# Reloads of gates and o in the W_A stage of blocks 1 and 2 tied to the ends of products

## The chip, the cores and the metric

The kernel runs on one core of one Trainium2 chip. The metric is the time of one execution on the device, in microseconds (us). All times of single instructions come from one profiled execution, counted from the start of its span.

## What is computed

One layer of a hybrid encoder is applied to a prompt of 2048 tokens and to a sample of 64 tokens, with 1024 features each, in float32. What matters here is the end of the layer:

```python
yA = einsum(silu(zA) * bA * conv, w_a_out)           # stage W_A
o  = o * rsqrt(mean(o * o) + EPS) * g_onorm          # o: result of the recurrent scan
yB = einsum(o * silu(zB), w_b_out)                   # stage W_B
merged = sigmoid(gA) * yA + sigmoid(gB) * yB
out = einsum(merged, w_o)                            # stage W_O
x = x + rms_norm(out, g_post)
x = x + (p @ w_ple_proj) * sigmoid(rms_norm(x, g_ple) @ w_ple_gate)
```

Ahead of it stand one wide projection `h @ w_in` with ten parts (vA, bA, cA, zA, q, f, iv, zB, gA, gB), a short convolution and the scan. gA, gB and the gated o are computed early in a block and used late.

## The kernel before

The 2112 tokens are cut into three blocks of 704 (blocks 0, 1, 2), each into two halves of 352. Activations lie as feature by token: eight tiles of 128 x 704 make one operand of 1024 features. Every matmul is 128 x 128 by 128 x 352. To keep float32 accuracy each operand is split in a high and a low part, and each product is made of three matmuls (high by high, high by low, low by high); splits are a cast on ScalarE and a subtraction on VectorE (`split`, L184 and L185).

Large matrix products are made by a Strassen scheme (Winograd's form): a 2 x 2 arrangement of weight blocks and activation blocks, seven products instead of eight. In the W_A and W_B stages of blocks 1 and 2 (`merge_in_turn`, `in_turn`) the seven products are run one after the other, in the order of `IN_TURN`: product 0 is A11 by B11, then 1: A12 by B21, 2: S2 by T2, 3: S3 by T3, 4: A22 by T4, 5: S1 by T1, 6: S4 by B22. One product runs over four groups of output features (g = 0 to 3); each group takes four k-steps of three matmuls, so 12 matmuls in a group and 48 in a product. While product n runs, `prepare` splits the operands of product n + 1, one k-step after each group, in `operand_of`, which for T2 also makes the sums of the scheme in place (L404 to L408).

The weights of a group come by SyncE's queue: a raw block or one of the precomputed sums S (256 KB, L195) is loaded to one of 5 `raw` tiles and cast on ScalarE to its high part (4 `hi` tiles). The low part is either loaded as well (256 KB, L216, to one of 4 `lo` or 3 `s` tiles), or, for the blocks listed under `anew` (A11 and A12 of W_A, A11 of W_B), computed on chip by L184 and L185, always to a `lo` tile. A tile is free again when its last reader is done, so a load runs ahead of TensorE by as many groups as there are tiles.

Results of a product go to the sinks: `sink_a` multiplies by the reloaded gate gA (tiles `m`), `sink_b` by gB (tiles `mg`) and adds `m`. Sinks run at products 1, 4, 5 and 6. The gates gA and gB, o and some others were spilled to memory earlier in the block (8 tiles of 352 KB each) and are brought back by `reload` (L929 to L932), a DMA that GpSimd issues (its line is L931) into one of 52 ring tiles. `loads` says when: gA 0 to 3 ahead of product 0, gA 4 to 7 after product 0, all of o after product 2, all of gB after product 5 of W_A. o is the operand of W_B. "After" is a place in the program's text: a scheduler orders each engine's instructions by their estimated times, and semaphores keep only what the data and the tiles need. On the chip a reload starts as soon as GpSimd reaches it and its ring tile is free, whatever TensorE is at.

Engines take their instructions in order, each from a queue of its own. GpSimd (POOL) issues the reloads and the spills and does few small computations; SyncE (SP) issues the weight loads. Both kinds of transfer run on the same 16 DMA engines.

Of the kernel before, what the change touches and what calls it, by code (L numbers as in the profile page):

```python
# [20 lines left out]
KB = D // P  # L21
KH = KB // 2
# [9 lines left out]
VA, BA, CA, ZA, QQ, FF, IV, ZB, GA, GB = range(10)  # L32
W_A, W_B, W_O, W_G = 80, 88, 96, 104
# [49 lines left out]
def hybrid_step(  # L83
# [17 lines left out]
    V, A, G, T, SP = nc.vector, nc.scalar, nc.gpsimd, nc.tensor, nc.sync  # L101
# [17 lines left out]
    def rt(n=BN, dt=F32):  # L119
        t = ring.tile([P, BN + 4], dt, tag="r", name=nm("r"))  # L120
        return t if n is None else t[:, :n]
# [112 lines left out]
    last, hooks = [None], []  # L234

    def placed():

        return tc.issue_after(last[0]) if last[0] is not None else nullcontext()

    def hook():  # L240

        if hooks:
            step = hooks.pop(0)
            if step is not None:
                step()
# [131 lines left out]
    def half(t, h):  # L377
        return t[:, h * HN : (h + 1) * HN]

    def whole(x, y):  # L380

        if y is None:
            return x
        t = hf()
        V.tensor_tensor(t, x, y, ALU.add)
        return t
# [102 lines left out]
    def gemm_late(idxs, act, segs):  # L489

        ws = [load_w(i) for i in idxs]
        pss = [[ps_gemm() for _ in segs] for _ in idxs]
        for ks in (range(KB - 1), (KB - 1,)):
            with placed() if len(ks) == 1 else nullcontext():
                for row, w in zip(pss, ws):
                    for ps, s in zip(row, segs):
                        for k in ks:
                            mm3(ps, w, act, k, cols_of(s))
        return pss
# [37 lines left out]
    def spread(cols, n):  # L537

        pb = ps_attn()
        with placed():  # L540
            for i, o in tiles_of(n):
                T.matmul(pb[:, o : o + P], cols[:, i : i + 1].to_broadcast([P, P]), ident, start=True, stop=True)
        return pb[:, :n]
# [8 lines left out]
    def col_rstd(acc, n):  # L552

        pc = ps_attn()
        cols = cols_tile(n)
        with placed():
            for i, o in tiles_of(n):
                T.matmul(pc[:, i : i + 1], acc[:, o : o + P], ones, start=True, stop=True)
        rstd_of(pc[:, : cols.shape[1]], cols, 1.0 / D)
        return cols  # L560
# [365 lines left out]
            yield  # L926


    def reload(d):  # L929
        t = rt()  # L930
        G.dma_start(t, d)  # L931
        return t  # L932

    def merge(bl, a, kept, extra):

        segs = bl["segs"]
        ob, m, mg, loaded = [], [], [], {}

        def fetch(kind, j):
            if j < KB:  # L940
                loaded[kind, j] = reload(kept[kind, j])

        fetch(GA, 0)
        fetch("o", 0)
        for j, pss in enumerate(gemms(W_A, a, segs)):
            fetch(GA, j + 1)
            fetch("o", j + 1)
            if j == KB - 1:
                fetch(GB, 0)
            sg = loaded.pop((GA, j))  # L950
            for s, ps in zip(segs, pss):
                V.tensor_tensor(sg[:, cols_of(s)], ps, sg[:, cols_of(s)], ALU.mult)
            m.append(sg)
            ob.append(split_rt(loaded.pop(("o", j))))
            if j % 2:
                next(extra, None)
        for j, pss in enumerate(gemms(W_B, ob, segs)):
            fetch(GB, j + 1)
            sg = loaded.pop((GB, j))
            for s, ps in zip(segs, pss):  # L960
                V.tensor_tensor(sg[:, cols_of(s)], ps, sg[:, cols_of(s)], ALU.mult)
            V.tensor_tensor(sg, sg, m[j], ALU.add)  # L962
            mg.append(split_rt(sg))
            if j % 2:
                next(extra, None)
        return mg

    def merge_in_turn(a, kept, mg, made):

        ob, m = [], []  # L970

        def gated(v, x, y):
            V.tensor_tensor(v, whole(x, y), v, ALU.mult)

        def sink_a(g, c, h, x, y):
            gated(half(m[g + c * KH], h), x, y)

        def sink_b(g, c, h, x, y):
            j = g + c * KH
            gated(half(mg[j], h), x, y)  # L980
            V.tensor_tensor(half(mg[j], h), half(mg[j], h), half(m[j], h), ALU.add)
            made(j, h)

        def loads(idx, n):

            if (idx, n) in ((W_A, -1), (W_A, 0)):
                m.extend(reload(kept[GA, j]) for j in range(len(m), len(m) + KH))
            elif (idx, n) == (W_A, 2):
                ob.extend(reload(kept["o", j]) for j in range(KB))
            elif (idx, n) == (W_A, 5):  # L990
                mg.extend(reload(kept[GB, j]) for j in range(KB))

        return [
            dict(idx=W_A, raw=a, sink=sink_a, anew=("A11", "A12")),
            dict(idx=W_B, raw=ob, sink=sink_b, anew=("A11",)),
        ], loads
# [105 lines left out]
    for bi, bl in enumerate(blocks):  # L1102
        first, kept = bi == 0, kepts[bi]
# [24 lines left out]
        mg, xo, h2, acc = [], [], [], rt()  # L1128
        if first:
            mg = merge(bl, a, kept, sums_ahead)  # L1130
        else:
            parts = [None] * KB

            def made(j, h):

                if nxt:
                    if parts[j] is None:
                        parts[j] = rt(dt=F32R), rt(dt=F32R)
                    split(half(mg[j], h), *(half(t, h) for t in parts[j]))
# [12 lines left out]
            if nxt:  # L1152
                mg = parts
# [69 lines left out]
```

## Time and profile before

| What | us |
|---|---|
| median of 3 runs | 2730.09 |
| the three runs | 2727.76, 2732.46, 2730.09 |
| the profiled execution, its own time | 2728.34 |
| its span, first to last instruction | 2726.6 |
| mean granted clock of TensorE over the span | 0.987 |
| W_A of block 1, first matmul | 1584.33 |
| W_A of block 2, first matmul | 2450.47 |

How to read the lines below. In an order in time a line gives start, duration, engine, source line, operation, written and read tiles, shapes, count, and in brackets the idle time before it with what ended it. In a view by stretches, a line gives for each engine the busy time and the number of instructions, then TensorE's granted clock as a share of full speed, the mean busy share of the 16 DMA engines, and GB/s. In the DMA views, q0 is GpSimd's queue and q1 SyncE's; a line of issues has the count, the size of each and the median time from issue to landing. TensorE's matmuls are pipelined: their starts tell the pace, not their durations.

### The profile page before, as it was taken

To read this page: it belongs to the slowest core of one execution; us is meant where nothing else is said; L and a number is where in the kernel's file an instruction comes from. 1 tells how busy PE (TensorE), PEld (TensorE's weight loads), DVE (VectorE), ACT (ScalarE), POOL (GpSimd) and SP (SyncE) were. 2 spreads that over 40 slices of the span, in tenths; PEclk is the share of its full clock that TensorE was granted. 3 is DMA by queue.
4 is the path that set the end of the run, shared out by engine and by line. 5 is a ranking of instruction groups with operands and counts; after the bars stand their busy time and mean duration, and the time that the engine had idled before them with its cause. 6 is when DMAs were issued, how large, how long until landed. Compare 5 with 4: busy or idle time off the path is not lost.

```text
span 2726.6 us, 47857 instructions
## 1 busy us (share of the span) xinstructions
PE 2646.6 (97%) x16736; PEld 2610.7 (96%) x16736; DVE 1721.8 (63%) x3327; ACT 1457.9 (53%) x2796; POOL 367.9 (13%) x684
## 2 busy tenths in 40 slices
PE   6999999999999999999999999999999999999998
PEld 5999999999999999999999999999999999999988
DVE  6788888899666643566645567554355554357864
ACT  4665565454324553566654556454466654445654
POOL 1000001100332211011111210021010010010022
PEclk7999999999999999999999999999999999999999
DMA  5767777898988898766789998598866678888878
GB/s 200 268 239 275 260 243 278 280 314 291 346 312 288 305 340 271 243 224 223 232 279 335 390 335 259 180 349 306 268 224 219 217 225 269 272 290 305 280 240 313
DMA packets 365681, 748.90 MB, mean 275 GB/s; under 512 B 44704, under 2 KB 48320, under 8 KB 365440
## 3 DMA queue, kind: packets, MB, share of 16 engines
q1 hardware_dynamic: 325728, 589.84, 64.9%
q0 software_dynamic: 39424, 155.96, 15.6%
q8 instruction: 132, 2.16, 0.3%
q14 instruction: 109, 0.89, 0.1%
q10 hardware_dynamic: 288, 0.05, 0.0%
HBM read 538.29 MB, written 207.37 MB: 273 GB/s over the span
## 4 chain that ended last, share of the span: by engine, by line
PE 78%; DMA 8%; DVE 4%; issue 4%; ACT 2%; POOL 1%; SPq 0%; DVEq 0%; POOLq 0%; ACTq 0%
PE pg L345 17%; PE pg L346 17%; PE pg L347 17%; PE pg L472 3%; PE pg L473 3%; PE pg L471 3%; PE pg L438 3%; PE pg L439 3%; PE pg L440 3%; DMA raw<-w_blk 2%; DMA raw<-S 1%; PE pa L826 1%; PE pa L862 1%; PE pa L864 1%; PE pa L816 1%
## 5 line engine op out<-in xcount | busy, mean ns | idle before, releaser
L345 PE MATMUL pg<-r,hi 128*128 128x352 f32 x3360 | 1115.1, 333 | 15.9 <-ACT r L184 5.9
L346 PE MATMUL pg<-r,hi 128*128 128x352 f32 x3360 | 1090.4, 325 | 5.0 <-DVE r L185 5.0
L347 PE MATMUL pg<-r,lo 128*128 128x352 f32 x2400 | 779.9, 325 | 4.8 <-DMA lo<-low 3.5
L215 ACT CAST hi<-raw 128x512 fp32r<-128x512 f32 x740 | 455.9, 619 | 589.7 <-PE pg L346 216.3
L345 PEld LDWEIGHTS pg<-r,hi 128*128 128x128 f32 x3360 | 634.8, 189 | 26.8 <-ACT r L184 8.9
L346 PEld LDWEIGHTS pg<-r,hi 128*128 128x128 f32 x3360 | 635.6, 189 | 9.6 <-DVE r L185 9.5
L347 PEld LDWEIGHTS pg<-r,lo 128*128 128x128 f32 x2400 | 454.0, 189 | 7.0 <-DMA lo<-low 4.7
L347 PE MATMUL pg<-r,s 128*128 128x352 f32 x960 | 310.5, 324 | 0.4 <-DMA s<-low 0.3
L472 PE MATMUL pg<-r,hi 128*128 128x352 f32 x896 | 291.9, 326 | 2.6 <-DVE r L185 2.3
L471 PE MATMUL pg<-r,hi 128*128 128x352 f32 x896 | 290.3, 326 | 1.8 <-ACT r L184 1.7
L473 PE MATMUL pg<-r,lo 128*128 128x352 f32 x728 | 237.5, 326 | 8.3 <-DVE lo L185 7.2
L184 ACT CAST r<-r 128x352 fp32r<-128x352 f32 (+2 forms) x294 | 162.8, 589 | 144.0 <-DVE r L962 43.3
L184 ACT CAST hi<-raw 128x512 fp32r<-128x512 f32 (+1 forms) x232 | 138.1, 597 | 181.2 <-PE pg L346 44.1
L185 DVE TENSOR_TENSOR r<-r,r 128x352 fp32r<-128x352 f32 (+2 forms) x294 | 183.6, 650 | 60.7 <-ACT r L184 60.0
L185 DVE TENSOR_TENSOR lo<-raw,hi 128x512 fp32r<-128x512 f32 (+1 forms) x232 | 152.2, 660 | 73.2 <-ACT hi L184 66.8
L438 PE MATMUL pg<-r,hi 128*128 128x352 f32 x560 | 182.6, 330 | 7.9 <-ACT r L184 7.9
L439 PE MATMUL pg<-r,hi 128*128 128x352 f32 x560 | 183.9, 330 | 0.9 <-DVE r L185 0.6
L347 PEld LDWEIGHTS pg<-r,s 128*128 128x128 f32 x960 | 180.4, 188 | 1.3 <-DMA s<-low 1.3
L472 PEld LDWEIGHTS pg<-r,hi 128*128 128x128 f32 x896 | 169.9, 190 | 4.5 <-DVE r L185 4.3
L184 ACT CAST hi<-s 128x512 fp32r<-128x512 f32 x160 | 98.8, 619 | 139.7 <-PE pg L346 137.0
L471 PEld LDWEIGHTS pg<-r,hi 128*128 128x128 f32 x896 | 169.6, 190 | 3.3 <-ACT r L184 2.9
L361 ACT COPY hf<-pg 128x352 f32<-128x352 f32 x360 | 158.3, 446 | 0.6
(327 smaller groups left out, 3991.7 us busy)
## 6 DMA issues: line engine op xcount, KB each, us to landing
raw<-w_blk SPq DMA_DIRECT2D x588, 256.0 KB, 4.0
lo<-low SPq DMA_DIRECT2D x422, 256.0 KB, 3.9
raw<-S SPq DMA_DIRECT2D x400, 256.0 KB, 4.0
low<-lo SPq DMA_DIRECT2D x344, 256.0 KB, 3.7
s<-low SPq DMA_DIRECT2D x318, 256.0 KB, 3.8
S<-s SPq DMA_DIRECT2D x160, 256.0 KB, 3.3
r<-x_fm POOLq DMA_DIRECT2D x40, 352.0 KB, 7.0
r<-w_blk POOLq DMA_DIRECT2D x48, 256.0 KB, 7.2
```

The lines of the kernel that those rows point to most:

```text
L184: A.copy(hi, src)
L185: V.tensor_tensor(lo, src, hi.bitcast(F32), ALU.subtract)
L215: A.copy(hi, raw)
L345: add(hi[:, k, :], xhi, start=start and k == 0, stop=False)
L346: add(hi[:, k, :], xlo, start=False, stop=False)
L347: last[0] = add(lo[:, k, :], xhi, start=False, stop=k == KH - 1).ins
L361: copied = A.copy(got[n], ps[bank])
L438: add(hi[:, k, :], xhi, start=start and k == 0, stop=False)
L439: add(hi[:, k, :], xlo, start=False, stop=False)
L471: T.matmul(ps, hi[:, k % 4, :], xhi[:, c], start=k == 0, stop=False)
L472: T.matmul(ps, hi[:, k % 4, :], xlo[:, c], start=False, stop=False)
L473: last[0] = T.matmul(ps, lo[:, k % 4, :], xhi[:, c], start=False, stop=k == KB - 1).ins
```

## The change

`reload` can make its DMA depend on the instruction in `last[0]`, which is the last matmul that the program has issued so far. All reloads in the W_A stage but the first four gates are made so, and o and gB are split in two sets of four:

| reload | placed before | placed after the change | waits for the last matmul of |
|---|---|---|---|
| gA 0 to 3 | ahead of product 0 | the same | nothing new |
| gA 4 to 7 | after product 0 | the same | product 0 |
| o 0 to 3 | after product 2 | the same | product 2 |
| o 4 to 7 | after product 2 | after product 3 | product 3 |
| gB 0 to 3 | after product 5 | the same | product 5 |
| gB 4 to 7 | after product 5 | after product 6 | product 6 |

```diff
+    def paced(dma):
+        tc.add_manual_dep(
+            dma.ins, last[0].name, mybir.DependencyInfo(mybir.DependencyClass.Sync, mybir.DependencyReason.DATA), reason="paced"
+        )
...
-    def reload(d):
+    def reload(d, pace=False):
         t = rt()
-        G.dma_start(t, d)
+        dma = G.dma_start(t, d)
+        if pace:
+            paced(dma)
         return t
...
         def loads(idx, n):
-            if (idx, n) in ((W_A, -1), (W_A, 0)):
-                m.extend(reload(kept[GA, j]) for j in range(len(m), len(m) + KH))
-            elif (idx, n) == (W_A, 2):
-                ob.extend(reload(kept["o", j]) for j in range(KB))
-            elif (idx, n) == (W_A, 5):
-                mg.extend(reload(kept[GB, j]) for j in range(KB))
+            if (idx, n) == (W_A, -1):
+                m.extend(reload(kept[GA, j]) for j in range(KH))
+            elif (idx, n) == (W_A, 0):
+                m.extend(reload(kept[GA, j], True) for j in range(KH, KB))
+            elif (idx, n) in ((W_A, 2), (W_A, 3)):
+                ob.extend(reload(kept["o", j], True) for j in range(len(ob), len(ob) + KH))
+            elif (idx, n) in ((W_A, 5), (W_A, 6)):
+                mg.extend(reload(kept[GB, j], True) for j in range(len(mg), len(mg) + KH))
```

Other uses of `reload` are unchanged. The scheduler lays out VectorE, ScalarE, TensorE and SyncE anew from its estimates, so some instructions of W_A and W_B change places on these engines; their numbers don't change.

## The prediction

> **What bounds the kernel now.** I read the page first, then windows of 20 us around the two places the diff touches (the W_A stage of block 1, from 1584 us, and of block 2, from 2450 us), then TensorE's waits and the order in time of single instructions there.
>
> ```profile
> span 2726.6 us, 47857 instructions
> PE 2646.6 (97%) x16736; PEld 2610.7 (96%) x16736; DVE 1721.8 (63%) x3327; ACT 1457.9 (53%) x2796; POOL 367.9 (13%) x684
> ```
>
> TensorE is busy for 97% of the span. The matmuls are unchanged, so the only thing to win is time in which it stands still or runs at a lower clock.
>
> ```profile
> 1580.00:1600.00 20.00, 15.65 (x86) 14.04 (x85) 14.24 (x29) 8.15 (x17) 4.27 (x8) 0.89 0.99 379
> 1600.00:1620.00 20.00, 20.00 (x109) 20.00 (x109) 11.03 (x25) 11.01 (x24) 4.24 (x8) 0.85 0.80 276
> 1620.00:1640.00 20.00, 20.00 (x126) 20.00 (x125) 14.96 (x33) 12.49 (x28) 0.00 (x0) 1.00 0.99 355
> 2460.00:2480.00 20.00, 16.52 (x84) 15.29 (x85) 12.14 (x26) 9.64 (x21) 2.13 (x4) 0.83 0.83 283
> 2480.00:2500.00 20.00, 20.00 (x126) 20.00 (x125) 12.68 (x27) 14.24 (x32) 2.12 (x4) 1.00 1.04 390
> ```
>
> The first brackets count matmuls, the last three columns are granted clock, DMA share and GB/s. An undisturbed slice holds 126 matmuls (159 ns each); the slices at 1580, 1600 and 2460 hold 86, 109 and 84, at clocks of 0.89, 0.85 and 0.83. In front of them, or in them, the DMA is full (0.99). So each block has one hole at the start of W_A. What makes it:
>
> ```profile
> 1584.33 0.32 PE L438 MATMUL pg<-r,hi 128*128 128x352 f32 x1
> 1593.52 0.43 PE L439 MATMUL pg<-r,hi 128*128 128x352 f32 x1 [0.43 <-DVE r L185]
> 1597.34 0.66 PE L438 MATMUL pg<-r,hi 128*128 128x352 f32 x1 [3.23 <-ACT r L184]
> 1601.27 0.49 PE L439 MATMUL pg<-r,hi 128*128 128x352 f32 x1
> 1601.57 0.49 PE L440 MATMUL pg<-r,lo 128*128 128x352 f32 x1
> 1606.22 0.33 PE L440 MATMUL pg<-r,lo 128*128 128x352 f32 x1
> 1606.38 0.32 PE L438 MATMUL pg<-r,hi 128*128 128x352 f32 x1
> ```
> ```profile
> 1595.93 0.62 ACT L184 CAST hi<-raw 128x512 fp32r<-128x512 f32 x1 [3.33 <-DMA raw<-w_blk]
> 1596.80 0.49 ACT L184 CAST r<-r 128x352 fp32r<-128x352 f32 x1
> ```
>
> Product 0 begins at 1584.33; its 48 matmuls end 7.7 us later, at 1592.1, and product 1 stops within its first four operands. The operand cast (ACT L184, r) that it waits for stands behind a weight cast (hi<-raw), and that one waits 3.33 us for a weight from memory. After the pause matmuls start 0.30 us apart (1601.27, 1601.57) until 1605.9, then 0.16 apart again. In block 2 the pauses are shorter and the slow stretch is there too:
>
> ```profile
> 2450.47 0.33 PE L438 MATMUL pg<-r,hi 128*128 128x352 f32 x1
> 2459.87 0.43 PE L438 MATMUL pg<-r,hi 128*128 128x352 f32 x1 [1.00 <-ACT r L184]
> 2462.07 0.43 PE L438 MATMUL pg<-r,hi 128*128 128x352 f32 x1 [1.06 <-ACT r L184]
> 2465.75 0.96 PE L438 MATMUL pg<-r,hi 128*128 128x352 f32 x2 [2.16 <-ACT r L184]
> ```
>
> Why the weight is late is in GpSimd's order in time and in the DMA view of 1573 to 1592 (issues, KB each, median us to landing):
>
> ```profile
> 1573.33 0.54 POOL L931 DMA_DIRECT2D r<-g__2815_11256  x1
> 1577.47 0.54 POOL L931 DMA_DIRECT2D r<-g__2927_11756  x1 [0.42 <-ACT hi L215]
> 1588.53 0.54 POOL L931 DMA_DIRECT2D r<-o  x1 [0.59 <-PE pg L440]
> ```
> ```profile
> q0 software_dynamic: 1033, 4.57, 63.0%
> q1 hardware_dynamic: 1240, 2.25, 36.3%
> r<-o POOLq DMA_DIRECT2D x8, 352.0 KB, 9.6
> raw<-w_blk SPq DMA_DIRECT2D x6, 256.0 KB, 11.3
> r<-g__2815_11256 POOLq DMA_DIRECT2D x1, 352.0 KB, 5.4
> r<-g__2927_11756 POOLq DMA_DIRECT2D x1, 352.0 KB, 10.5
> ```
>
> All 16 reloads of 352 KB (8 gates, 8 o) go out between 1573.3 and 1589.1: 16 x 0.36 = 5.8 MB, 63% of the DMA time there, and the weights of product 1 take 11.3 us. In a calm stretch (1630 to 1650) the same load takes 2.9:
>
> ```profile
> raw<-w_blk SPq DMA_DIRECT2D x8, 256.0 KB, 2.9
> lo<-low SPq DMA_DIRECT2D x3, 256.0 KB, 4.7
> ```
>
> **The change part by part.** *Removed from the hole.* Gates 4 to 7 wait for product 0's last matmul, o 0 to 3 for product 2's, o 4 to 7 for product 3's. So only the first four gates (1.4 MB, landing from 5.4 us on) share the DMA with product 1's weights; 12 x 0.36 = 4.3 MB leave the stretch, at some 380 GB/s (the slice's 379) 11 us of transfers. The weight cast of 1595.93 then comes when its buffer is free, and product 1 runs on. The price of the hole I take from the first result of product 2, which VectorE picks up:
>
> ```profile
> 1610.92 0.52 DVE L449 TENSOR_TENSOR r<-r,pg 128x352 f32<-128x352 f32 x1 [0.52 <-PE pg L440]
> 2475.92 0.52 DVE L449 TENSOR_TENSOR r<-r,pg 128x352 f32<-128x352 f32 x1 [0.50 <-PE pg L440]
> ```
>
> From the first matmul of product 0 to that point lie 48 + 48 + 12 = 108 matmuls. Undisturbed they take 107 x 0.161 (7.73 / 48) + 0.32 for the last + 0.07 to VectorE = 17.6 us. Block 1 takes 1610.92 - 1584.33 = 26.6, block 2 2475.92 - 2450.47 = 25.45: 9.0 and 7.85 lost. A changeover of this form keeps about 0.1 us of wait (the same kind of changeover in W_B, 1657, shows no named wait), so 8.9 + 7.7 = **16.6 us** go.
>
> The clock is the larger half of it. In block 2 the three pauses are 1.00 + 1.06 + 2.16 = 4.2, so 3.5 us come from the slow stretch. [...] Here the rows decide: the slow stretch follows the pauses directly in both blocks.
>
> *Added: a wait on GpSimd's queue.* Behind the waiting reloads stand only the next reloads; then, in block 1, the x loads (first at 1692) and in block 2 the p loads (2527), long after product 6. No vector or TensorE work passes that queue. Nothing: 0. The instruction counts of all engines stay (the order of GpSimd's stays, word for word); no instruction is added.
>
> *Moved: 4 reloads to each of five points* (GB 0 to 3 after product 5, GB 4 to 7 after product 6). Each must land before its use. The shortest notice is GB 0 to 3: product 6, W_B's product 0 and a quarter of its product 1, 2 x 7.7 + 1.9 = 17 us; the slowest landing above is 10.5. Cost 0. The other side is what each burst does to the weights beside it. Before has a burst of four in steady running, gates of GB at 2472.8 to 2474.9; the DMA view of 2472 to 2476 and of the next one, 2480 to 2484:
>
> ```profile
> lo<-low SPq DMA_DIRECT2D x3, 256.0 KB, 6.5
> s<-low SPq DMA_DIRECT2D x1, 256.0 KB, 8.5
> ```
>
> TensorE paid nothing for these (126 matmuls in 2480 to 2500), since low halves are usually fetched some 11 us ahead. But where a product follows one whose low halves are made on chip (W_A product 1, W_B product 0; those hold all four lo tiles), the first low half that gets a lo tile can only be fetched when the first group of the product before is done. In the built program that is the first group of W_B's product 1 in both blocks and of W_A's product 2 in block 2: notice 7.73 - 1.93 + 0.3 = 6.1 us, and a burst starts just there (gates 4 to 7; GB 4 to 7). In block 1's product 2 it is the second group, 8 us. With the calm 4.7 us the cost is 0, with 6.5 it is 0.4, with 8.5 it is 2.4 a place. I take 6.5, the row of a single burst: 3 x 0.45 = **1.4 us**. A short pause leaves the clock alone here:
>
> ```profile
> 1774.56 0.43 PE L345 MATMUL pg<-r,hi 128*128 128x352 f32 x1 [0.90 <-ACT hf L361]
> 1772.00:1782.00 10.00, 8.40 (x53) 7.51 (x53) 5.68 (x10) 5.47 (x10) 0.33 (x1) 1.00 0.50 158
> ```
>
> *Moved on VectorE and ScalarE* by the scheduler, which now counts on o later: the splits of o (first L185, then the sums L404, L407) go from products 5 and 4 to the end of product 6 and W_B's product 0. At the changeover, behind the last matmuls of product 6, VectorE has in turn: a weight's low half (0.61 from start to start), one sum (L385, 0.44), then the low half of the fourth o operand (0.52). From ScalarE's cast 0.1 us after product 0 of W_B starts, it is ready 2.35 us after that start. TensorE's own order has been moved too: 14 matmuls (14 x 0.161 = 2.25) now stand ahead of it. Left: **0.1 us** a block, 0.2 in all. In W_B's product 0 eighteen VectorE steps of 0.44 lead to the last operand of product 1: ready 10.1 us after the start, wanted after 7.8 + 15 x 0.161 = 10.2. Cover just suffices; without it, each step that is late costs 0.44.
>
> Sum: -16.6 + 1.4 + 0.2 = **-15.0 us**. The profiled execution took 2728.34 us (span 2726.6 and 1.7 around it): 2713.3. It lies 1.75 below the median of the runs, 2730.09; from the median the sum gives 2715.1. I forecast **2714**.
>
> **The rivals.** *Only half of it goes.* One block's hole stays because four early gates suffice to delay product 1's weights, or the places above wait 2.4 us each. For it: product 1's weights are the first after the gates. Against: 1.4 MB at 380 GB/s is gone in 4 us, and ScalarE can't use these weights before product 0's first group ends. Time: 2728.3 - 7.7 or - 16.6 + 7.4, so 2719 to 2721.
>
> *Slower: the bursts starve the low halves.* If a first low half lands 8.5 us after issue where it has 6.1, TensorE pauses 2.4 us and, as in block 2 now, loses 3.5 more at the low clock: 5.9 a place. Break-even is 16.6 / 5.9 = 2.8 places; with all four (block 1's product 2 too) 2728.3 - 16.6 + 23.6 + 0.2 = 2735.5. For it: DMA is at 0.8 to 1.0 in these slices, so each burst pushes something. Against: 8.5 us was seen with two bursts 8 us apart, and 0.90 us of pause left the clock at 1.00.
>
> *It doesn't do what it says, or early was right.* If the waits release early, all 16 reloads go out as now: 2728, no change. That the reloads now land too late is excluded by 17 us of notice against 10.5. [...]
>
> **How the numbers follow.** The forecast (2708 to 2717) has 0.68, the half 0.14, no change (waits void, or two to three starved places, 2725 to 2734) 0.09, slower 0.09. About 0.2%, 5.5 us, is what a measurement of this kernel can tell from no change. So faster 0.82, same 0.09, slower 0.09. The range takes the forecast and the half: 2708 (no new wait gives 2711.7; the three runs spread over 4.7 us, most of which I allow below it) to 2724.
>
> **What would show it.** Right: in block 1 the reloads of gates 4 to 7 are issued about 1592.3, o about 1607.8 and 1615.5; the weights of product 1 land in under 6 us; product 2's first result comes 17.7 us after product 0's first matmul; the granted clock is 1.00 throughout W_A. Wrong: TensorE waits for lo<-low at the first groups of product 2 or of W_B's product 1, with the clock below 1.00 behind them; or pauses of over 0.5 us for r (L185) at the start of W_B.

## The result, and the profile after

The changed kernel takes 2722.04 us (median of 9 runs, 2717.35 to 2727.44), the kernel before beside it 2732.46 us (9 runs, 2727.76 to 2739.95). The ratio is 0.9966, with a 95% interval of 0.9954 to 0.9978: 9.3 us faster by the ratio, 10.4 by the medians, where 15.0 were forecast. The profiled execution took 2725.05 us with a span of 2723.4. Its span is only 3.2 us shorter than that of the profiled one of before, mostly since the code ahead of the change ran 4.5 us longer in it (W_A of block 1 begins at 1588.85, not at 1584.33). So the two traces are compared from the first matmul of W_A on, block by block.

The stretches of the changed kernel, with the columns of the prediction's fence (time, then busy time and count of TensorE, its weight loads, VectorE, ScalarE, GpSimd; clock, DMA share, GB/s):

```profile
1580.00:1600.00 20.00, 20.00 (x125) 19.77 (x125) 20.00 (x42) 11.33 (x24) 2.12 (x4) 1.00 0.76 249
1600.00:1620.00 20.00, 20.00 (x125) 20.00 (x125) 9.12 (x20) 11.70 (x25) 2.13 (x4) 1.00 1.00 362
1640.00:1660.00 20.00, 18.09 (x102) 17.59 (x102) 16.32 (x37) 9.36 (x21) 2.12 (x4) 0.91 0.89 327
2460.00:2480.00 20.00, 18.72 (x117) 18.43 (x116) 8.75 (x19) 11.33 (x25) 2.12 (x4) 1.00 0.94 338
2500.00:2520.00 20.00, 18.84 (x116) 18.33 (x115) 18.60 (x42) 11.90 (x26) 2.24 (x5) 1.00 0.99 347
```

The slices that held 86 and 109 matmuls hold 125 each, at a clock of 1.00, and the DMA share of the first fell from 0.99 to 0.76. The hole is gone. But the slices at 1640 and 2500 now hold 102 and 116, and the one at 2460, which held 84, holds 117 and not 126. Before, the first two were whole:

```profile
1640.00:1660.00 20.00, 20.00 (x126) 19.76 (x125) 16.79 (x36) 10.37 (x22) 0.00 (x0) 1.00 0.74 226
2500.00:2520.00 20.00, 20.00 (x126) 20.00 (x125) 18.39 (x40) 9.48 (x19) 0.00 (x0) 1.00 0.71 221
```

The list of all of TensorE's waits says the same in one line for each kernel (what it waited for: total us, times, longest). First before, then after:

```profile
PE pg L438 <- ACT r L184: 7.9, 5, 3.2
```
```profile
PE pg L446 <- DMA lo<-low: 4.3, 3, 1.9
```

The in-turn matmuls (L438 to L440 before, L444 to L446 after) no longer wait for the operand cast; they wait three times for a low half of a weight. The order in time of the changed kernel, at both ends of the old hole and at the three waits:

```profile
1588.85 0.32 PE L444 MATMUL pg<-r,hi 128*128 128x352 f32 x1
...
1606.61 0.52 DVE L455 TENSOR_TENSOR r<-r,pg 128x352 f32<-128x352 f32 x1 [0.48 <-PE pg L446]
...
1653.47 0.43 PE L446 MATMUL pg<-r,lo 128*128 128x352 f32 x1 [1.91 <-DMA lo<-low]
...
1655.37 0.50 PE L445 MATMUL pg<-r,hi 128*128 128x352 f32 x1
1655.66 0.50 PE L446 MATMUL pg<-r,s 128*128 128x352 f32 x1
...
2465.22 0.43 PE L446 MATMUL pg<-r,lo 128*128 128x352 f32 x1 [1.28 <-DMA lo<-low]
...
2513.34 0.43 PE L446 MATMUL pg<-r,lo 128*128 128x352 f32 x1 [1.16 <-DMA lo<-low]
```

From product 0's first matmul to product 2's first result block 1 takes 1606.61 - 1588.85 = 17.76 us (26.6 before). The waits stand at product 1 of W_B in block 1, product 2 of W_A in block 2, product 1 of W_B in block 2. Behind the first one the matmuls go 0.29 apart for some 3 us.

GpSimd's order shows that the reloads go out where the change puts them, and the two DMA views of the changed kernel, 1578 to 1597 (beside product 0) and 1643 to 1651 (the start of W_B), show what each meets (queue: packets, MB, share of the DMA engines' time; issues: count, KB each, median us to landing):

```profile
1597.03 0.54 POOL L937 DMA_DIRECT2D r<-g__2891_11593  x1 [17.06 <-PE pg L446]
...
1612.71 2.13 POOL L937 DMA_DIRECT2D r<-o  x4 [13.56 <-PE pg L446]
1620.48 2.12 POOL L937 DMA_DIRECT2D r<-o  x4 [5.64 <-PE pg L446]
...
1643.67 0.54 POOL L937 DMA_DIRECT2D r<-g__3063_12295  x1 [5.61 <-PE pg L446]
```
```profile
q1 hardware_dynamic: 1895, 3.44, 56.6%
q0 software_dynamic: 352, 1.45, 21.1%
...
raw<-w_blk SPq DMA_DIRECT2D x6, 256.0 KB, 5.4
```
```profile
q0 software_dynamic: 309, 1.39, 50.2%
q1 hardware_dynamic: 775, 1.41, 48.6%
...
lo<-low SPq DMA_DIRECT2D x3, 256.0 KB, 7.2
```

Beside product 0 the reloads' share fell from 63% to 21%, and a weight takes 5.4 us where it took 11.3. At the start of W_B the four gB reloads of 1643.67 have half of the DMA time, and a low half takes 7.2.

### The profile page after: what moved, and what is told of

Read it like the earlier page. It is cut to its first block, busy times and chain, and to the rows that moved or that the text cites. A ratio compares the mean times of both kernels' runs of the same rounds, so it can differ in the third digit from the quotient of the medians.

```text
span 2723.4 us, 47821 instructions
## 1 busy us (share of the span) xinstructions
PE 2643.9 (97%) x16736; PEld 2607.7 (96%) x16736; DVE 1719.6 (63%) x3327; ACT 1458.2 (54%) x2796; POOL 368.9 (14%) x684
## 4 chain that ended last, share of the span: by engine, by line
PE 79%; DMA 8%; issue 5%; DVE 3%; POOL 2%; ACT 1%; SPq 0%; POOLq 0%; DVEq 0%; ACTq 0%
PE pg L351 18%; PE pg L352 17%; PE pg L353 17%; PE pg L444 3%; PE pg L446 3%; PE pg L445 3%; PE pg L478 3%; PE pg L479 3%; PE pg L477 3%; DMA raw<-w_blk 1%; DMA raw<-S 1%; PE pa L868 1%; PE pa L832 1%; PE pa L870 1%; PE pa L822 1%
## 5 line engine op out<-in xcount | busy, mean ns | idle before, releaser
L185 DVE TENSOR_TENSOR r<-r,r 128x352 fp32r<-128x352 f32 (+2 forms) x294 | 183.9, 648 | 61.3 <-ACT r L184 60.8
L185 DVE TENSOR_TENSOR lo<-raw,hi 128x512 fp32r<-128x512 f32 (+1 forms) x232 | 151.6, 658 | 65.1 <-ACT hi L184 53.3
L444 PE MATMUL pg<-r,hi 128*128 128x352 f32 x560 | 180.2, 326 | 0.0
```

The costliest lines, as they stand in the source:

```text
L185: V.tensor_tensor(lo, src, hi.bitcast(F32), ALU.subtract)
L444: add(hi[:, k, :], xhi, start=start and k == 0, stop=False)
```

## The experiments

Theory 1: the 12 reloads held back remove the hole, and the bursts of four give part of it back, because a burst lengthens the way of a low half that has short notice. Theory 2: the gain comes from the new order of VectorE's and ScalarE's instructions. Theory 3: the new waits come from the short notice alone, whatever the reloads do. "Block time" below is from the first to the last in-turn matmul of block 1 (W_A, W_B) and of block 2 (W_A, W_B, W_O), in the profiled executions, and "hole" the time from product 0's first matmul to product 2's first result, 17.8 when undisturbed. Ratios are to the kernel before, run beside each on the same chip.

| kernel | median, us | ratio, 95% interval | hole, blocks 1, 2 | block time 1 + 2 |
|---|---|---|---|---|
| before | 2732.46 | 1 | 26.6, 25.5 | 117.7 + 172.6 |
| after | 2722.04 | 0.9966 [0.9954, 0.9978] | 17.8, 19.3 | 112.7 + 168.1 |
| e1_places | 2733.54 | 1.0001 [0.9992, 1.0010] | 26.3, 27.1 | 117.5 + 174.2 |
| e3_gb_late | 2717.82 | 0.9942 [0.9930, 0.9955] | 17.8, 19.0 | 109.2 + 167.3 |
| e4_ga_late | 2722.51 | 0.9965 [0.9953, 0.9978] | 17.8, 17.8 | 114.6 + 170.1 |
| e5_both_late | 2719.75 | 0.9953 [0.9940, 0.9965] | 17.8, 17.8 | 110.6 + 167.0 |
| e6_gb_doubled | 2730.32 | 0.9996 [0.9986, 1.0006] | 17.8, 19.9 | 111.3 + 174.6 |
| e7_low_tiles | 2715.44 | 0.9948 [0.9933, 0.9963] | 17.8, 17.8 | 109.2 + 165.6 |
| e8_low_tiles_gb_late | 2716.19 | 0.9947 [0.9932, 0.9962] | 17.8, 17.8 | 109.1 + 167.0 |
| e2_o_only | 2733.65 | 1.0012 [1.0002, 1.0021] | 20.6, 19.0 | 118.8 + 174.2 |
| e9_before_tiles | 2719.98 | 0.9953 [0.9940, 0.9967] | 19.3, 18.2 | 110.4 + 165.3 |
| e10_after_again | 2722.54 | 0.9958 [0.9942, 0.9974] | 17.8, 19.4 | 114.5 + 168.8 |
| e11_low_tiles_again | 2718.05 | 0.9946 [0.9933, 0.9958] | 17.8, 17.8 | 110.1 + 165.5 |
| e12_lows_late | 2737.15 | 1.0021 [1.0007, 1.0035] | 19.6, 19.4 | 122.1 + 177.3 |

**The places without the waits (e1_places).** All six places of the change, but no reload waits for a product.

```diff
-                m.extend(reload(kept[GA, j], True) for j in range(KH, KB))
+                m.extend(reload(kept[GA, j], False) for j in range(KH, KB))
```
(and the same for o and gB)

> All reloads at the places of the change (o and gB in two sets), but none waits for a product. Theory 1 (the gain comes from keeping 12 reloads out of the transfers beside product 1's weights): the reloads go out as early as in the kernel before, the hole at product 1 of W_A is back (8 to 9 us in block 1, 7 to 8 in block 2), time as before, 2730 to 2734. Theory 2 (the gain comes from the new order that the scheduler gives VectorE and ScalarE once o is placed later): at least half of the gain stays, 2727 or less.

The whole gain is gone, ratio 1.0001, and the hole is back at 26.3 and 27.1. Theory 2 falls: what the changed places do to the order gains nothing without the waits.

**Bursts moved away from the low halves (e3_gb_late, e4_ga_late, e5_both_late).** In e3 gB 4 to 7 stand after product 1 of W_B, in e4 gA 4 to 7 after product 1 of W_A, and e5 does both.

```diff
-            elif (idx, n) in ((W_A, 5), (W_A, 6)):
+            elif (idx, n) in ((W_A, 5), (W_B, 1)):
```
```diff
-            elif (idx, n) == (W_A, 0):
+            elif (idx, n) == (W_A, 1):
```

> As the change, but gates gB 4 to 7 are placed after product 1 of W_B and wait for it, instead of product 6 of W_A. Theory 1 (the new waits for low halves come from a burst of four reloads that starts just where the first low half is fetched on short notice): both waits for lo<-low in product 1 of W_B go (1.91 us with the slow matmuls behind it in block 1, 1.16 in block 2), the one of 1.28 in product 2 of W_A of block 2 stays; 4 to 5 us less than the change, about 2717. Theory 3 (the notice is too short by itself, since a lo tile comes free late; the burst does nothing): all three waits stay, 2722.

> As the change, but gates gA 4 to 7 are placed after product 1 of W_A and wait for it, instead of product 0. Theory 1: the wait of 1.28 us for lo<-low in product 2 of W_A of block 2 goes, the two in W_B stay (about 1.9 and 1.2 us); 1 to 1.5 us less than the change, 2720 to 2721. Theory 3: nothing changes, all three waits stay, 2722.

> Both: gA 4 to 7 after product 1 of W_A, gB 4 to 7 after product 1 of W_B, each waiting for it. Theory 1: no wait for lo<-low over 0.3 us in W_A and W_B, granted clock 1.00 throughout; 5.5 to 6.5 us less than the change, 2715 to 2717, some 16 us less than the kernel before. Theory 3: 2722 as the change.

e3 took what theory 1 says: 2717.82. Its list of waits has one low half left, that of W_A in block 2, whose burst it left alone:

```profile
PE pg L446 <- DMA lo<-low: 0.9, 1, 0.9
```

The notice of W_B's low halves in block 1 was the same, only the burst was elsewhere, so theory 3 falls: the first one was issued 3.0 us after W_B's first matmul in both kernels (1646.17 - 1643.20 in the changed one, 1645.85 - 1642.87 in e3), and took 7.2 us to land in the changed kernel, 4.3 in e3. e4 and e5 are half misses. The low half at product 2 has no wait any more (hole 17.8 in block 2), but the scheduler laid out VectorE and ScalarE anew, and TensorE now waits at the start of W_B for an operand's low half (r, L185): 1.02 and 0.53 us in e4, 0.97 and 1.14 in e5. In e4 the two waits for low halves in W_B, which its edit leaves alone, came out longer as well (2.11 and 1.75 us), and in block 2 half pace followed, which it did not in the changed kernel: the slice from 2500 has a clock of 0.91. e4 gains nothing and e5 less than e3.

**The burst doubled (e6_gb_doubled).** All eight gB wait for product 6.

```diff
-            elif (idx, n) in ((W_A, 5), (W_A, 6)):
-                mg.extend(reload(kept[GB, j], True) for j in range(len(mg), len(mg) + KH))
+            elif (idx, n) == (W_A, 6):
+                mg.extend(reload(kept[GB, j], True) for j in range(KB))
```

> All eight gB wait for product 6, so that the burst beside the first low half of W_B's product 1 has 8 reloads and not 4; nothing else is moved. Theory 1 (the wait grows with the burst): the waits of 1.91 and 1.16 us at product 1 of W_B become 3.5 to 5 each, with a slow stretch of the clock behind both, so 5 to 9 us on the changed kernel's 2722: 2727 to 2731. Theory 3 (short notice without the burst): the waits stay at 1 to 2 us, 2722.

The time rose by 8 us to 2730.32, as theory 1 has it. The DMA view of e6 over 2501 to 2509 and TensorE's order there:

```profile
q0 software_dynamic: 433, 1.99, 66.7%
q1 hardware_dynamic: 398, 0.74, 29.6%
...
lo<-low SPq DMA_DIRECT2D x4, 256.0 KB, 10.4
```
```profile
2513.33 0.66 PE L446 MATMUL pg<-r,lo 128*128 128x352 f32 x1 [3.60 <-DMA lo<-low]
2513.79 0.49 PE L444 MATMUL pg<-r,hi 128*128 128x352 f32 x1
2514.08 0.49 PE L445 MATMUL pg<-r,hi 128*128 128x352 f32 x1
```

With eight reloads beside it a low half takes 10.4 us, and the wait in block 2 is 3.60 with half pace right behind it. In block 1 the wait did not grow: 0.28 us, with 1.29 for an operand cast ahead of it. Its first low half landed 7.2 us after its issue there, no later than in the changed kernel; those behind it took 9.0 to 10.0. That half of the expectation missed, and why the first came through stays open.

**More notice, bursts as they are (e7_low_tiles, e8_low_tiles_gb_late).** The low halves made on chip go to lo and s tiles in turn, as the loaded ones do, and no longer all to lo. e7 is the changed kernel with that, e8 is e3 with that.

```diff
-    def split_w(raw, key=None):
+    def split_w(raw, key=None, spread=False):
...
-        lo = wp.tile([P, 4, P], F32R, tag="lo", name=nm("lo"))
+        lo = low_tile() if spread else wp.tile([P, 4, P], F32R, tag="lo", name=nm("lo"))
...
-            return split_w(load_raw(w_blk[keys[name]]), None if anew else keys[name])
+            return split_w(load_raw(w_blk[keys[name]]), None if anew else keys[name], anew)
```

> The changed kernel with the reloads where they are, but the low halves that are made on chip in W_A and W_B are spread over lo and s tiles in the same turn as the loaded ones, so that the first loaded low half of the next product gets its tile some groups earlier: the notice grows from 6 to about 10 us or more, the bursts stay. Theory 1 (burst against notice): the three waits for lo<-low (1.91, 1.28, 1.16 us) go, and with them the slow stretch in block 1: 2722 - 6 = 2716, range 2714 to 2719. A rival: the tile isn't what sets the issue, and the waits stay at 2722.

> The same spread of low halves over lo and s tiles, with gB 4 to 7 also moved behind product 1 of W_B as in the best run so far (2717.8, where only the wait of 0.90 us at product 2 of W_A in block 2 was left). Theory 1: that last wait goes too, 2717.8 - 1 = 2717; no less than the run with the tiles alone, since each remedy takes the same W_B waits.

As expected: 2715.44 and 2716.19. The same three slices of e7, and its DMA view at the start of W_B (1640 to 1647):

```profile
1640.00:1660.00 20.00, 20.00 (x122) 19.40 (x122) 19.61 (x44) 12.33 (x27) 2.12 (x4) 1.00 1.01 359
2460.00:2480.00 20.00, 20.00 (x126) 20.00 (x126) 7.50 (x16) 11.21 (x24) 4.24 (x8) 1.00 1.04 392
2500.00:2520.00 20.00, 19.90 (x123) 19.49 (x122) 19.45 (x46) 16.71 (x38) 1.07 (x2) 1.00 1.02 376
```
```profile
lo<-low SPq DMA_DIRECT2D x3, 256.0 KB, 7.8
```

A low half takes 7.8 us, longer than in the changed kernel, and TensorE waits for none: the notice covers it. The three slices hold 122, 126 and 123 matmuls where the changed kernel had 102, 117 and 116; 36 x 0.159 = 5.7 us is what the bursts cost it in these two traces, and the block times differ by 280.8 - 274.8 = 6.0.

**One part alone (e2_o_only).** Only o waits; gA and gB go out as before the change.

> One part alone: only o waits (for products 2 and 3); gates 4 to 7 go out freely after product 0's place and all of gB after product 5's, as before the change. Of the 12 reloads held back from the hole 8 (o) are still held, and 8 gates stand beside product 1's weights where the change has 4. Theory 1 (weights late by the bytes queued beside them): the weights of product 1 land after some 7 to 9 us, TensorE pauses 1 to 2 us at product 1 of each block where it paused 3 to 4 in all, and the W_A wait of block 2's product 2 goes with the burst; W_B's too, since gB goes out in one piece while product 5 or 6 runs: 2718 to 2724, between before (2732) and the best so far (2718). Theory 3 (short notice by itself): W_B's waits for lo<-low stay.

A miss: 2733.65, no gain at all. The hole did shrink, to 20.6 and 19.0, with eight gates beside product 0. Most of the loss is at the end of W_A, in product 6 of block 1 and in products 5 and 6 of block 2. GpSimd's order, the DMA view of 1623 to 1636 and TensorE's order show it for block 1:

```profile
1623.34 2.12 POOL L937 DMA_DIRECT2D r<-o  x4 [5.63 <-PE pg L446]
1625.46 0.54 POOL L937 DMA_DIRECT2D r<-g__2973_11945  x1
```
```profile
s<-low SPq DMA_DIRECT2D x3, 256.0 KB, 14.4
```
```profile
1641.41 0.42 PE L446 MATMUL pg<-r,s 128*128 128x352 f32 x1 [2.31 <-DMA s<-low]
```

The gB reloads wait for nothing of their own, but stand behind o in GpSimd's queue. They go out the moment o 4 to 7 are through: twelve reloads within 12 us (1623.3 to 1635.4). The low halves issued beside them, those of W_A's last products, take some 14 us in block 1, and TensorE waits 7.5 us for four of them in the two blocks (in block 1 the 2.31 above and 1.43 one group later). In block 2 half pace follows (the slice from 2500 has a clock of 0.83), and in W_B TensorE waits 2.4 us more in both blocks together for low halves of operands (r, L185). The pile has moved, not gone.

**The tiles without the change (e9_before_tiles).** The edit of e7 on the kernel before, all reloads early.

> The kernel before, with only the spread of the chip-made low halves over lo and s tiles, and the reloads as they were. Theory 1 (the tiles only help against the bursts of the change): the hole at product 1 of W_A stays, 8 to 9 us a block, and the time stays at before's, 2731, range 2727 to 2734. Rival (the tiles have a gain of their own, and the run of the changed kernel with them isn't about the bursts): 2724 to 2726.

A miss that changes the story: 2719.98, ratio 0.9953, as good as the change, with all 16 reloads where they were. The hole is 19.3 and 18.2. The first reload goes out 11.0 us ahead of W_A's first matmul, as in the kernel before. So the reloads alone do not make it. What differs is in SyncE's order ahead of W_A of block 1. The kernel before:

```profile
1572.92 0.32 SPq L216 DMA_DIRECT2D s<-low  x1
1573.46 2.95 SPq L195 DMA_DIRECT2D raw<-w_blk  x2
1576.78 0.38 SPq L216 DMA_DIRECT2D s<-low  x1
1577.32 3.14 SPq L195 DMA_DIRECT2D raw<-w_blk  x2
1580.64 0.33 SPq L216 DMA_DIRECT2D s<-low  x1
1582.04 2.23 SPq L195 DMA_DIRECT2D raw<-w_blk  x2
```

Between the weights of products 0 and 1 stand three low halves for products 2 and 3. They are fetched over 25 us before their use, because products 0 and 1 of before use no s tile and leave all three free. In block 2 three stand in the same way (2441.01, 2444.87, 2448.75). In e9 the s tiles are taken, and these three loads come later. The changed kernel still has the three (1577.44 and these two) and no hole:

```profile
1581.29 0.33 SPq L216 DMA_DIRECT2D s<-low  x1
...
1585.15 0.33 SPq L216 DMA_DIRECT2D s<-low  x1
```

New theory: the hole needs both, reloads that hold two thirds of the DMA and low halves that stand ahead of product 1's weights in SyncE's queue. That queue moved 2.25 MB in the 19 us of the prediction's DMA view, 118 GB/s, so 3 x 0.26 = 0.79 MB ahead of a weight are up to 6.6 us.

**Those three loads later (e12_lows_late).** The kernel before, where all low halves of products 2 and 3 of W_A (eight in a block, the three among them) wait for the cast of their own weight. The order of TensorE, VectorE, ScalarE and GpSimd is that of before, word for word; only SyncE's differs.

```diff
+        after_cast = lambda dma, cast, key: key[1] in ("S2", "S3") and W_A <= key[0] < W_A + KH and tc.add_manual_dep(dma.ins, cast.ins.name, mybir.DependencyInfo(mybir.DependencyClass.Sync, mybir.DependencyReason.DATA), reason="late")
...
-            A.copy(hi, raw)
-            SP.dma_start(lo.bitcast(F32), lows[key])
+            cast = A.copy(hi, raw)
+            after_cast(SP.dma_start(lo.bitcast(F32), lows[key]), cast, key)
```

> The kernel before, its reloads as they were, every tile as it was, and the instructions of TensorE, VectorE, ScalarE and GpSimd in the same order: only the low halves of W_A's products 2 and 3 that SyncE fetches ahead (three of them, 0.79 MB, issued between the weights of products 0 and 1) wait for the cast of their own weight, and so leave the queue in which product 1's weights stand. New theory (the hole needs both: reloads that take about two thirds of the DMA, and low halves ahead of the weights in SyncE's queue, which moves about a third of 380 GB/s there, so 0.79 MB of it are about 5.7 us): the weights of product 1 land about 5 us earlier, the hole shrinks from 8 to 9 us a block to 0 to 2, less up to 1 us for a low half that now comes late at product 2: 2714 to 2722. Theory 1 alone (the reloads): the hole stays, 2731. A rival on the run with the tiles spread (its gain came from the tiles of the chip-made halves): 2731 as well.

The hole did what the new theory says: 19.6 and 19.4, with all 16 reloads early. The weight for which ScalarE had waited 3.33 us comes in time, in e12 and in e9 (first e12):

```profile
1594.35 0.62 ACT L184 CAST hi<-raw 128x512 fp32r<-128x512 f32 x1 [0.84 <-DMA raw<-w_blk]
```
```profile
1593.42 0.62 ACT L184 CAST hi<-raw 128x512 fp32r<-128x512 f32 x1 [0.89 <-DMA raw<-w_blk]
```

Counted from product 0's first matmul it is cast after 11.6 us in before (1595.93 - 1584.33), 7.3 in e12 (1594.35 - 1587.05) and 7.0 in e9 (1593.42 - 1586.41). The total missed: 2737.15, 5 us above before. The loads held back now have too little notice: the first of them goes out 13.3 us after product 0's first matmul (1600.35 - 1587.05), where the three of before went out 3.7 to 11.4 us ahead of it. TensorE waits 13.6 us for five of them in products 2 and 3; the first wait:

```profile
1611.90 0.43 PE L440 MATMUL pg<-r,s 128*128 128x352 f32 x1 [3.10 <-DMA s<-low]
```

**Again, side by side (e10_after_again, e11_low_tiles_again).** The changed kernel and e7 once more on one chip.

> The changed kernel once more, to stand beside the next one on the same chip: 2722, ratio to before 0.9966.

> The changed kernel with the low halves spread over lo and s tiles, once more, as the best version: 2715.5, ratio to before 0.9948, 6 to 7 us below the changed kernel.

2722.54 and 2718.05: 4.5 us apart, less than the 6 to 7 expected, in the same direction. The two ratios' intervals overlap; what shows the gain of the tiles is the waits that are gone in both profiles. The waits of the changed kernel stand at the same three places; that of block 1 is 3.6 us here, where it was 1.91, since its low half took 9.0 us and not 7.2. So one wait of one kernel differs by 1.7 us from run to run. The best versions, e3, e5, e7, e8, e9 and e11, lie within 0.9942 to 0.9953 with intervals that overlap. I do not rank them.

## Why the prediction was right, and where not

*The time: inside the range, but not by the sum.* The measured 2722.04 lies above 2708 to 2717, which had 0.68, in the part of the range that was taken in for the rival "only half of it goes" (0.14). Of the 8 us above 2714, 4.6 are the sum (15.0 forecast, 10.4 measured), 2.4 the kernel before, which took 2732.46 beside the changed one and not 2730.09, and 1.1 the step from 2715.1 to 2714. That the range held is the rival's doing and not the forecast's.

*The hole: right in place and size.* 8.9 and 7.7 were to go. Block 1 went from 26.6 to 17.76 (8.8), and its 17.76 stands against the 17.6 + 0.1 worked out. Block 2 went to 19.34; without the new wait of 1.28 and what follows it, it is 17.8 (e4, e5, e7): 7.65. The clock was 1.00 through W_A of both blocks, so the slow stretch did hang on the pauses. "The clock is the larger half" goes too far: TensorE's named waits in the hole are 4.3 us of 9.0 in block 1 and 4.2 of 7.85 in block 2, so pauses and slow stretch took about half each. In block 1 the slow stretch began at 1595.57, within the pause of 3.23 us, in block 2 at 2462.56, behind the pauses of 1.00 and 1.06 us and ahead of the longest.

*The cause of the hole: only half of it.* The prediction puts it on the reloads. The three early low halves in the same queue as the weights are the other half: taking either away shrinks it to 0 to 2 us (after, with the low halves early and the reloads late; e9 and e12, with the reloads early and the low halves late). The DMA view that the prediction quotes (1573 to 1592) held the other half in a row that it left out:

```profile
s<-low SPq DMA_DIRECT2D x3, 256.0 KB, 9.9
```

The prediction counted the bytes in q0 and never asked what else stood in q1.

*GpSimd's waits at 0: right.* In the changed kernel TensorE waits for no reload in W_A or W_B. e2 shows when a wait there isn't free: with unpaced reloads behind it.

*Three places x 0.45 = 1.4 us: the term that failed.* The places were right, all three and no fourth; the sum was 6 us. Both the notice and the way of a low half were mis-sized. SyncE's order in the changed kernel has the three issues:

```profile
1646.17 0.33 SPq L216 DMA_DIRECT2D lo<-low  x1
...
2458.34 0.32 SPq L216 DMA_DIRECT2D lo<-low  x1
...
2506.74 0.32 SPq L216 DMA_DIRECT2D lo<-low  x1
```

TensorE wanted them at 1653.47 - 1.91 = 1651.56, at 2463.94 and at 2512.18: a notice of 5.4, 5.6 and 5.4 us, not 6.1. It went on 7.3, 6.9 and 6.6 us after the issue, not 6.5. So the notice was 0.5 to 0.7 us shorter and the way 0.1 to 0.8 us longer than counted, which makes 0.45 into 1.2 to 1.9. The bounds given (0 to 2.4 a place) held here, the value chosen from them did not (in the second run of the changed kernel one wait was 3.6); and "a short pause leaves the clock alone" failed at the longest of the three, behind which 11 matmuls went 0.29 apart and not 0.16, about 1.5 us more.

*VectorE's changeover, 0.1 a block: right.* No wait for r (L185) is named at the start of W_B in the changed kernel. The cover is as thin as said: in e4 and e5 another order of the same instructions costs 0.5 to 1.1 us there.

With the terms as measured: -8.8 - 7.65 + 6.0 = -10.5 us, against 290.3 - 280.8 = 9.5 from the block times and 10.4 from the medians; the 1 us between the terms and the block times is not assigned. The rival "only half of it goes" named the right mechanism beside the forecast, the low halves, at 2.4 a place, and its 7.4 us were nearer to the 6.0 than the 1.4 chosen. "Early was right", which gave no change, did not come true: 10.4 us went. But e9 gains as much with every reload early, so it is not the early issue as such that costs, but what it meets in the queues.

## What to carry to other kernels

A late transfer had two causes here, what shared the engines with it and what stood ahead of it in its own queue: with either taken away the hole fell from 26.6 and 25.5 us to between 17.8 and 19.6. So look at the issues of its own queue before you move the other queue's. Count tiles as notice: the same bursts cost some 6 us with one rotation of the low tiles, where the notice was 5.4 to 5.6 us and a low half took 6.6 to 7.3, and no wait with the other, where a low half took 7.8. And a wait put on one reload held back all reloads behind it, which then came together: twelve within 12 us in e2, and low halves beside them took 14.4 us.

## What the runs showed of the hardware

*With two queues busy the packets were about one to one, the bytes were not.* From 1581 to 1595 of before, with reloads and weights on their way all the time, q0 moved 878 packets and 3.95 MB and q1 890 packets and 1.63 MB; in e2 from 1628 to 1642 it was 875 and 3.94 against 879 and 1.60, in e6 from 2501 to 2509 433 and 1.99 against 398 and 0.74. At 4.5 KB a packet against 1.8 KB (MB by packets, in before) the reloads had 71 to 73% of the two queues' bytes in these views. Where one queue is nearly alone for part of a view the counts differ: 1643 to 1651 of the changed kernel has 309 and 775, of which q1 moved 493 and q0 13 up to 1645.5.

*The length of one pause did not tell whether the clock fell.* 1.91 us in the changed kernel was followed by half pace 1.3 us later, its slice at 0.91. In block 1 of e2 pauses of 2.31 and 1.43 us, 3.6 us apart, left the slice at 1.00. The stretches at half clock in the W_A and W_B stages lasted 10.24 us (block 1, from 1595.57) and 6.83 us (block 2, from 2462.56) in before and 3.41 us in the changed kernel. In stretches of that last length, the changed kernel from 1651.17 and e2 from 1637.26 read:

```profile
1651.17:1654.58 3.41, 1.50 (x10) 1.22 (x9) 3.04 (x7) 1.31 (x3) 0.00 (x0) 1.00 1.04 394
1654.58:1658.00 3.42, 3.42 (x13) 3.42 (x12) 0.63 (x2) 0.62 (x1) 0.00 (x0) 0.50 0.47 175
```
```profile
1637.26:1640.67 3.41, 1.84 (x12) 1.54 (x10) 0.48 (x2) 0.97 (x2) 0.00 (x0) 1.00 1.04 398
1640.67:1644.08 3.41, 2.19 (x12) 1.90 (x12) 1.11 (x3) 0.35 (x1) 0.00 (x0) 1.00 1.02 383
```

The 1.91 us lie in the first stretch of the changed kernel and leave TensorE idle for 3.41 - 1.50 = 1.91 us of it; the next one runs at 0.50. The 2.31 us of e2 lie in two stretches, with 1.57 and 1.22 us idle, and the clock stays at 1.00. In before TensorE was idle for 1.90 and 1.96 us of the 3.41 ahead of its two stretches at half clock (1592.16 to 1595.57 and 2459.15 to 2462.56), the second with no named pause longer than 1.06. So a pause of about 2 us cost some 1.5 us beyond its own length in the changed kernel and no slow matmuls in block 1 of e2. What decides between the two was not shown.
